# Bank assignment of score tiles and value products in the memory attention of a hybrid encoder step

## The chip, the cores and the metric

The kernel runs on one core of one Trainium2 chip. The metric is the device time of one execution in microseconds (us); the time given for a kernel is the median of its runs. A profile is one further execution, recorded by the hardware profiler; its span runs from the first to the last recorded instruction.

Engine names as in the profile: PE is TensorE (matmuls), PEld its weight loads, DVE VectorE, ACT ScalarE, POOL GpSimd, SP the engine whose queue issues most DMAs. PSUM, where matmuls write, has eight banks of 512 float32 values per partition.

## The reference

One layer of an encoder is applied to 512 prompt tokens and 64 sample tokens, with shared weights: a mixing block (a gated delta recurrence beside a differential attention), a cross-attention to a memory of 256 rows, and a feed-forward block; then a final norm. The change concerns the cross-attention:

```python
def _mem_attn(x, mk, mv, wq, wo):                      # x: rmsnorm(h)
    q = (x @ wq).reshape(B, L, H_MEM, D_MEM)            # 4 heads of width 256
    s = jnp.einsum('blhd,bmhd->bhlm', q, mk) * (D_MEM ** -0.5)
    p = jax.nn.softmax(s, axis=-1)                      # over 256 memory rows
    o = jnp.einsum('bhlm,bmhd->blhd', p, mv)
    return o.reshape(B, L, D_MODEL) @ wo
```

For the prompt, mk and mv are projected from the memory input; for the sample they come from a cache.

## The kernel before, in words

**Layout.** Activations lie transposed: model dimension on the 128 partitions (eight blocks of 128), the 576 tokens along the free axis. A matmul of near-float32 accuracy is made of three matmuls on operands split into a high and a low part (float32r each): high by high, low weight by high, high weight by low. `project` (L169) computes one 128-wide block of outputs for all tokens in two halves: tokens 0 to 255 in one bank (eight contraction steps k; at each, the high weights go over the high and low activations side by side, 512 columns in one matmul, and the low weights over 256 columns), then tokens 256 to 575 (eight steps of three matmuls with 320 columns). A projection is thus 16 + 24 = 40 matmuls. Its weights arrive by DMA as `raw` (three buffers) and are split by ACT (`wh`, L161) and DVE (`wl`, L162), two buffers each.

**The memory attention** is a loop over four heads h (L1151 on). For each head:

- two projections give the head's queries, evacuated and split by `split_query` (high part L1160 on ACT, low part `ql` L1161 on DVE, both after L194 and L195 for the first half);
- five score tiles t, one for each 128 tokens of the prompt and one for the sample. A tile is six matmuls of 256 columns into a bank `gs`; then DVE takes the row maximum (L1178) and scales it (L1179), ACT takes the exponential and its sum out of the bank (L1181), DVE takes the reciprocal (L1182) and scales the row (L1183). The bank is free after the exponential. PE transposes the 128 by 256 probabilities as two blocks into a bank `ba` (L113); for a prompt tile ACT casts each block to its high part (L1190) and DVE subtracts to get the low part (L1191); for the sample tile DVE copies (L1193, tile `an` in the profile). The probability tile `p0` has two buffers;
- two value products i, one for each 128 of the head's 256 columns: six matmuls of 512 columns for the prompt tokens into `b`, four of 64 columns for the sample into `b2`; both are evacuated and split into the tile pair `mo` by ACT (L1209) and DVE (L1210).

After the loop, `project` is called for the eight blocks of w_mem_o over `mo` (the contraction steps k = 2h and 2h + 1 need head h), each followed by the residual add (`add_residual`, L1092 and L1094) and `combine`, which prepares operands of the feed-forward block. `split_first` and `load_pair` (L1262) prepare the first weights of that block on DVE, ACT and the DMA queue.

**Banks.** PSUM is given out by tag:

```python
BANKS = dict(pr=3, ba=2, g0=1, g1=1, gs=1)
```

A tag with n banks hands out n tiles in turn; the next tile waits until the oldest has been read for the last time. `project` uses `pr`, the transposes use `ba`, score tiles `gs`, value products `g0` and `g1`. The feed-forward block later uses `ba`, `gs` and `g1` for its seven products (`ff1_pair`).

**Order.** The framework puts each engine's instructions into one fixed order when the program is built, by simulating their costs: what comes earlier in the program has priority, and what is not ready yet lets later work pass. (The splitting of weights has a raised priority.) On the chip each engine runs its list in order, and an instruction whose operands or bank aren't ready holds up all behind it. So within head h PE's list mixes the head's score matmuls, transposes and value products with the projections of head h + 1, the next work in the program. In the last head, h = 3, there are no queries left to project; what can be mixed in are the first projections of w_mem_o, as far as their contraction steps k = 0 to 5 (heads 0 to 2) and the three `pr` banks reach.

Of the kernel before, what the change touches and what calls it, by code (L numbers as in the profile page):

```python
# [37 lines left out]
def hybrid_layer_kernel(  # L38
# [40 lines left out]
    def nm(s):  # L79
        uid[0] += 1  # L80
        return f"{s}_{uid[0]}"

    def pair(slot, dt=F32):

        return up.tile([P, 2, 4, T], dt, tag=f"u{slot}", name=nm("u"))
# [6 lines left out]
    def small(tag, shape, bufs=None, dt=F32):  # L92
        tag = SHARED.get(tag, tag)
        bufs = 1 if tag in ("vn", "on", "S") or tag[:-1] in ("At", "Dt", "Y") else 2
        return sp.tile(shape, dt, tag=tag, name=nm(tag), bufs=bufs)

    def tiny(shape, tag="tiny", bufs=16):
        return tp.tile(shape, F32, tag=tag, name=nm(tag), bufs=bufs)

    def bank(tag="ba"):  # L100
        return ps.tile([P, 512], F32, tag=tag, name=nm(tag), bufs=BANKS[tag])
# [4 lines left out]
    def mm(out, lhsT, rhs, start=True, stop=True, pin=False, skip_group_check=False):  # L106
        i = nc.tensor.matmul(out, lhsT, rhs, start=start, stop=stop, skip_group_check=skip_group_check)  # L107
        if pin:
            tc.keep_in_program_order(i)

    def tr(out, in_, pin=False):
        n = in_.shape[0]
        i = nc.tensor.transpose(out, in_, ident[:n, :n])  # L113
        if pin:
            tc.keep_in_program_order(i)
# [49 lines left out]
    def weights(w, c0, kt=KT):  # L165

        return split_weights(w[:, c0 : c0 + P], [P, kt, P])

    def project(w, x, evac, kt=KT, halves=HALVES, between=None):  # L169


        for a0, n in halves:
            b = bank("pr")
            for k in range(kt):
                low_part = lambda: mm(b[:, :n], w[1][:, k, :], x[k // 4][:, 0, k % 4, a0 : a0 + n], start=False, stop=False)
                if k == kt - 1:
                    low_part()
                high_parts(b, w[0], x, k, a0, n, kt)
                if k < kt - 1:
                    low_part()  # L180
            if between and a0 == 0:
                between()
            evac(b[:, :n], a0, n, None if a0 else b[:, 256:])
# [9 lines left out]
    def add_to(dst, b, more):  # L193
        A.copy(dst, more)  # L194
        V.tensor_tensor(dst, b, dst, ALU.add)  # L195
# [298 lines left out]
    for a0, n in HALVES:  # L494
        b = bank("pr")
# [7 lines left out]
    b = bank()  # L503
# [67 lines left out]
    for j in range(3):  # L571
        b = bank()
# [456 lines left out]
    def lows(*tags):  # L1029

        return [small(tag, [P, 512], dt=F32R) for tag in tags]
# [9 lines left out]
    for w, out in ((w_mem_k, o_mk), (w_mem_v, o_mv)):  # L1041
        dst = tokens
        for f in range(2):
# [17 lines left out]
            if out is o_mk:  # L1061
                for i in range(2):
                    b = bank()
# [79 lines left out]
    for k2 in range(KT // 2):  # L1143
        b = bank()
# [6 lines left out]
    for h in range(H):  # L1151
        qh = [small("kd" if h % 2 else "aT", [P, T], dt=F32R) for i in range(2)]
        ql = cp.tile([P, 2, T], F32R, tag=f"qz{h % 2}", name=nm("ql"))
        for i in range(2):
            def split_query(b, a0, n, more):
                if more is not None:
                    q = small("zr", [P, 320])[:, :n]
                    add_to(q, b, more)
                    b = q
                A.copy(qh[i][:, a0 : a0 + n], b)  # L1160
                V.tensor_tensor(ql[:, i, a0 : a0 + n], b, qh[i][:, a0 : a0 + n].bitcast(F32), ALU.subtract)  # L1161

            project(weights(w_mem_q[0], (2 * h + i) * P), hx, split_query)

        pT = [lows(*tags) for tags in ((("p1", "p1"), ("S", "vn")) if h % 2 else (("vb", "vb"), ("KQ", "KQ")))]
        pS = small("an", [P, 2, DEC])
        for t, (q0, _) in enumerate(QT):
            t0, n = TT[t]
            kk, kl = (mkT, mkl) if t < 4 else (cmT, cml)
            b = bank("gs")  # L1170
            for i in range(2):
                m, q = 2 * h + i, slice(q0, q0 + P)
                low_keys = kl[m // 2][:, m % 2, :]
                mm(b[:, :NMEM], qh[i][:, q], kk[:, m, :], start=i == 0, stop=False)
                mm(b[:, :NMEM], qh[i][:, q], low_keys, start=False, stop=False)
                mm(b[:, :NMEM], ql[:, i, q], kk[:, m, :], start=False, stop=i == 1)
            mx, l = tiny([P, 1]), tiny([P, 1])
            V.tensor_reduce(mx, b[:, :NMEM], AX.X, ALU.max)  # L1178
            V.tensor_scalar(mx, mx, shrink16[:, t : t + 1], None, ALU.mult)  # L1179
            p = small("p0", [P, 512])  # L1180
            A.activation(p[:, :NMEM], b[:, :NMEM], AF.Exp, bias=mx, scale=grow16[:, t : t + 1], accum_out=l)  # L1181
            V.reciprocal(l, l)  # L1182
            V.tensor_scalar(p[:, :NMEM], p[:, :NMEM], l, None, ALU.mult)  # L1183
            bt = bank()
            for bi in range(2):
                tr(bt[:, bi * P : (bi + 1) * P], p[:, bi * P : (bi + 1) * P])
            if t < 4:
                for bi in range(2):
                    src, (dh, dl) = bt[:, bi * P : (bi + 1) * P], (x[bi][:, t0 : t0 + n] for x in pT)
                    A.copy(dh, src)  # L1190
                    V.tensor_tensor(dl, src, dh.bitcast(F32), ALU.subtract)  # L1191
            else:
                V.tensor_copy(pS, bt[:, : 2 * P].rearrange("p (b n) -> p b n", b=2)[:, :, P - n :])  # L1193
        if h % 2 == 0:
            mo.append(pair(4 if h else 5, F32R))
        for i in range(2):
            b, b2 = bank("g0"), bank("g1")
            fs = slice((2 * h + i) * P, (2 * h + i + 1) * P)
            for bi in range(2):
                m = 2 * h + i  # L1200
                mm(b, mv[:, bi, fs], pT[0][bi], start=bi == 0, stop=False)
                mm(b, mv[:, bi, fs], pT[1][bi], start=False, stop=False)
                mm(b, mvl[2 * bi + m // 4][:, (m % 4) * P : (m % 4 + 1) * P], pT[0][bi], start=False, stop=bi == 1)
            for bi in range(2):
                mm(b2[:, :DEC], cmv[2 * bi + m // 4][:, (m % 4) * P : (m % 4 + 1) * P], pS[:, bi, :], start=bi == 0, stop=bi == 1)
            j = 2 * (h % 2) + i
            for src, ts_ in ((b, slice(0, SEQ)), (b2[:, :DEC], slice(SEQ, T))):
                dh, dl = (mo[h // 2][:, p, j, ts_] for p in range(2))
                A.copy(dh, src)  # L1209
                V.tensor_tensor(dl, src, dh.bitcast(F32), ALU.subtract)  # L1210
# [322 lines left out]
    for m in range(KT):  # L1533
# [3 lines left out]
        if m in (3, 4):  # L1537
            t = m - 3
# [43 lines left out]
```

## Time and profile before

| | us |
|---|---|
| median of 3 runs (lowest, highest) | 1025.71 (1025.43, 1027.94) |
| profiled execution, its own time | 1028.23 |
| its span | 1026.5 |
| PE busy in the span | 1003.6 (98%) |
| PE weight loads | 921.1 (90%) |
| DVE busy | 706.8 (69%) |
| ACT busy | 537.0 (52%) |
| POOL busy | 57.1 (6%) |
| memory attention, first score matmul to the wait behind the last value product | 485.42 to 574.41 |

The profiled execution lies 2.52 us above the median and 1.73 us above its own span. All times with a position, such as 551.1, are us from the start of the span. A row of the table of windows gives a stretch, its length and the busy time of each engine with the number of instructions, then the granted TensorE clock (PEclk, 1.00 is full speed). Ends of matmuls are modelled, so that two in sequence overlap in the listing; the distance from start to start is the pace. A bracket at a row's end is the engine's idle time before it and what ended it. The profile names tiles by their tag: `u` is the big activation pairs, `aT` and `kd` the high queries of even and odd heads, `g` the banks `g0` and `g1`.

### The profile page before, as it was taken

What the parts mean: (1) busy time and instruction counts of PE and PEld (TensorE: products, weight loads), DVE (VectorE), ACT (ScalarE), POOL (GpSimd) and SP (SyncE); (2) the same over time, 40 slices, a digit from 0 to 9 for tenths busy, and PEclk for the clock granted to TensorE, in tenths of its full rate; (3) what the DMA queues carried; (4) which work ended last, traced back from release to release, by engine and by line L of the source; (5) the groups of instructions that cost most, each with busy time, mean ns of one, the idle gap of its engine ahead of it and who ended that gap; (6) DMA issues with size and microseconds to landing.
All of it is one profiled execution on the core that took longest, in us unless ns stands there. A gap on an engine that the chain in (4) does not pass through costs nothing.

```text
span 1026.5 us, 17294 instructions
## 1 busy us (share of the span) xinstructions
PE 1003.6 (98%) x6630; PEld 921.1 (90%) x6630; DVE 706.8 (69%) x1529; ACT 537.0 (52%) x1170; POOL 57.1 (6%) x123
## 2 busy tenths in 40 slices
PE   9999999999999999999999999999999999999996
PEld 7989899998888877899988899999999999999986
DVE  6576785776566676665665787667766677777883
ACT  6654664343465665444444557655544555555434
POOL 3431010100000000000000000000000000000000
PEclk9999999999999999999999999999999999999998
DMA  7332320100312355523211233332222222222202
GB/s 217 122 104 78 107 74 21 44 21 22 104 53 75 100 177 189 172 84 115 62 42 42 62 114 93 114 93 83 83 83 83 83 83 83 82 83 83 82 1 93
DMA packets 121255, 89.99 MB, mean 88 GB/s; under 512 B 5507, under 2 KB 112129, under 8 KB 120661
## 3 DMA queue, kind: packets, MB, share of 16 engines
q1 hardware_dynamic: 120804, 88.24, 28.6%
q8 instruction: 52, 0.85, 0.3%
q10 hardware_dynamic: 368, 0.66, 0.2%
q14 instruction: 31, 0.25, 0.1%
HBM read 79.14 MB, written 9.74 MB: 87 GB/s over the span
## 4 chain that ended last, share of the span: by engine, by line
PE 84%; DVE 4%; issue 3%; ACT 3%; POOL 2%; DMA 1%; POOLq 0%; ACTq 0%; DVEq 0%; SPq 0%
PE pr L107 49%; PE g L107 14%; PE ba L107 10%; PE gs L107 7%; PE ba L113 2%; PE g L113 2%; DVE wl L162 0%; DMA raw<-in_w_ff_dram 0%; POOL tg L208 0%; DVE p L457 0%; DMA out_dram<-S 0%; DMA S<-in_state_gdn_dram 0%; POOL X L604 0%; DMA r<-in_w_ff_dram 0%; DVE on L780 0%
## 5 line engine op out<-in xcount | busy, mean ns | idle before, releaser
L107 PE MATMUL pr<-u,wh 128*128 128x320 f32 (+2 forms) x1240 | 328.2, 342 | 2.1 <-DVE p L323 1.0
L107 PEld LDWEIGHTS pr<-u,wh 128*128 128x128 f32 x1240 | 211.6, 188 | 18.6 <-DVE p L323 1.3
L107 PE MATMUL pr<-u,wl 128*128 128x256 f32 (+1 forms) x816 | 227.7, 303 | 0.0
L107 PEld LDWEIGHTS pr<-u,wl 128*128 128x128 f32 x816 | 149.7, 189 | 3.7 <-issue 0.7
L162 DVE TENSOR_TENSOR wl<-raw,wh 128x1024 fp32r<-128x1024 f32 x65 | 79.5, 1223 | 34.4 <-ACT wh L161 32.5
L107 PE MATMUL pr<-u,w2h 128*128 128x320 f32 (+1 forms) x384 | 99.2, 343 | 2.8 <-DVE u L1415 2.8
L161 ACT CAST wh<-raw 128x1024 fp32r<-128x1024 f32 x65 | 68.2, 1049 | 58.0 <-PE pr L107 52.2
L1330 ACT CAST w2h<-r 128x512 fp32r<-128x512 f32 x56 | 34.7, 620 | 93.6 <-PE pr L107 89.9
L107 PE MATMUL pr<-f,w2h 128*128 128x320 f32 (+1 forms) x288 | 73.8, 340 | 0.0
L107 PEld LDWEIGHTS pr<-u,w2h 128*128 128x128 f32 x384 | 65.9, 191 | 7.9 <-DVE u L1415 3.1
L107 PE MATMUL pr<-u,w2l 128*128 128x256 f32 (+1 forms) x256 | 65.8, 298 | 0.0
L1415 DVE TENSOR_TENSOR u<-u,pr 128x256 f32<-128x256 f32 x96 | 42.9, 449 | 18.5 <-PE pr L107 17.6
L107 PE MATMUL ba<-u,wl 128*128 128x288 f32 x360 | 52.9, 295 | 0.6 <-ACT keep L1366 0.5
L107 PEld LDWEIGHTS pr<-f,w2h 128*128 128x128 f32 x288 | 48.7, 188 | 4.2 <-issue 1.2
L107 PEld LDWEIGHTS ba<-u,wl 128*128 128x128 f32 x360 | 49.2, 188 | 1.2 <-ACT keep L1366 1.2
L107 PEld LDWEIGHTS pr<-u,w2l 128*128 128x128 f32 x256 | 47.5, 191 | 1.5
L107 PE MATMUL pr<-f,w2l 128*128 128x256 f32 (+1 forms) x192 | 48.8, 295 | 0.0
L1331 DVE TENSOR_TENSOR w2l<-r,w2h 128x512 fp32r<-128x512 f32 x56 | 38.5, 688 | 11.3 <-ACT w2h L1330 10.8
L208 POOL TENSOR_TENSOR tiny<-tiny,nhalf 128x1 f32<-128x1 f32 (+4 forms) x10 | 9.2, 924 | 633.7 <-DVE tiny L1479 542.0
L107 PE MATMUL pr<-wh,u 128*128 128x512 f32 x128 | 41.2, 400 | 0.0
L107 PEld LDWEIGHTS pr<-f,w2l 128*128 128x128 f32 x192 | 35.2, 188 | 1.1
L1375 ACT ACTIVATE c<-c 128x288 f32<-128x288 f32 x48 | 20.9, 442 | 28.1 <-DVE c L1374 28.1
(462 smaller groups left out, 2078.5 us busy)
## 6 DMA issues: line engine op xcount, KB each, us to landing
raw<-in_w_ff_dram SPq DMA_DIRECT2D x36, 512.0 KB
raw<-in_w_in_dram SPq DMA_DIRECT2D x28, 512.0 KB
r<-in_w_ff_dram SPq DMA_DIRECT2D x56, 256.0 KB
raw<-in_w_mem_k_dram SPq DMA_DIRECT2D x8, 512.0 KB
raw<-in_w_mem_v_dram SPq DMA_DIRECT2D x8, 512.0 KB
raw<-in_w_out_dram SPq DMA_DIRECT2D x8, 512.0 KB
raw<-in_w_mem_q_dram SPq DMA_DIRECT2D x8, 512.0 KB
raw<-in_w_mem_o_dram SPq DMA_DIRECT2D x8, 512.0 KB
```

What stands on the lines that cost most here:

```text
L107: i = nc.tensor.matmul(out, lhsT, rhs, start=start, stop=stop, skip_group_check=skip_group_check)
L113: i = nc.tensor.transpose(out, in_, ident[:n, :n])
L161: A.copy(wh, raw)
L162: V.tensor_tensor(wl, raw, wh.bitcast(F32), ALU.subtract)
L208: G.tensor_tensor(out, in_, bc(nhalf[: in_.shape[0], 0:1], list(in_.shape)), ALU.pow)
L1330: A.copy(wh, src)
L1331: V.tensor_tensor(wl, src, wh.bitcast(F32), ALU.subtract)
L1375: A.activation(c, c, AF.Relu)
L1415: V.tensor_tensor(am, am, b, ALU.add)
```

## The change

Two lines of the memory attention name other banks. The score tiles t = 0 to 4 of a head take `gs`, `g0`, `g1`, `gs`, `g0`. The value product i = 0 has its prompt part in `g0` and its sample part in `g1` as before; i = 1 has its prompt part in `gs` and its sample part in one of the two `ba` banks. No matmul, no instruction of another engine and no DMA is added or removed; `BANKS` stays as it is.

```diff
         for t, (q0, _) in enumerate(QT):
             t0, n = TT[t]
             kk, kl = (mkT, mkl) if t < 4 else (cmT, cml)
-            b = bank("gs")
+            b = bank(("gs", "g0", "g1")[t % 3])
             for i in range(2):
                 m, q = 2 * h + i, slice(q0, q0 + P)
                 low_keys = kl[m // 2][:, m % 2, :]
...
         if h % 2 == 0:
             mo.append(pair(4 if h else 5, F32R))
         for i in range(2):
-            b, b2 = bank("g0"), bank("g1")
+            b, b2 = bank(("g0", "gs")[i]), bank(("g1", "ba")[i])
             fs = slice((2 * h + i) * P, (2 * h + i + 1) * P)
             for bi in range(2):
                 m = 2 * h + i
```

## The prediction

> **What bounds the kernel now.** I read the page first: busy time by engine, then the chain that ended last.
>
> ```profile
> span 1026.5 us, 17294 instructions
> PE 1003.6 (98%) x6630; PEld 921.1 (90%) x6630; DVE 706.8 (69%) x1529; ACT 537.0 (52%) x1170; POOL 57.1 (6%) x123
> PE 84%; DVE 4%; issue 3%; ACT 3%; POOL 2%; DMA 1%; POOLq 0%; ACTq 0%; DVEq 0%; SPq 0%
> ```
>
> PE is busy 98% of the span and is 84% of the chain. The change removes no matmul, so it can only win where PE idles or runs slowly in the memory attention. The table of windows with one stretch for each head, cut at the head's first score matmul (the last ends behind PE's last wait), shows where that is:
>
> ```profile
> 485.42:507.20 21.78, 21.78 (x142) 19.77 (x141) 13.49 (x41) 10.59 (x30) 0.00 (x0) 1.00 0.17 49
> 507.20:529.10 21.90, 21.90 (x142) 19.79 (x141) 13.56 (x42) 10.57 (x30) 0.00 (x0) 1.00 0.17 49
> 529.10:550.98 21.88, 21.88 (x143) 19.74 (x141) 12.77 (x41) 10.54 (x30) 0.00 (x0) 1.00 0.17 49
> 550.98:574.41 23.43, 20.69 (x119) 17.46 (x117) 13.06 (x41) 9.22 (x27) 0.00 (x0) 0.93 0.07 23
> ```
>
> In heads 0 to 2 PE is busy all of the time at full clock: the next head's 80 projection matmuls fill every wait for a bank. Only head 3 has a hole: 23.43 - 20.69 = 2.74 us idle, and a clock of 0.93. PE's windows inside it and its listing tell what happens:
>
> ```profile
> 562.00:563.00 1.00, 0.09 (x1) 1.00 0.00 0
> 563.50:564.00 0.50, 0.34 (x2) 0.81 0.00 0
> 564.00:565.00 1.00, 1.00 (x6) 0.50 0.00 0
> 565.00:566.00 1.00, 0.86 (x4) 0.50 0.00 0
> 566.00:567.00 1.00, 1.00 (x3) 0.50 0.00 0
> 567.00:567.50 0.50, 0.50 (x3) 0.78 0.00 0
> ```
> ```profile
> 551.89 0.42 DVE L1178 TENSOR_REDUCE tiny<-gs 128x1 f32<-128x256 f32 x1 [0.15 <-PE gs L107]
> ...
> 560.82 0.39 PE L107 MATMUL gs<-u,kd 128*128 128x256 f32 x1
> ...
> 561.41 0.44 PE L113 MATMUL ba<-ident,p 128*128 128x128 f32 x2
> ...
> 562.13 0.42 DVE L1178 TENSOR_REDUCE tiny<-gs 128x1 f32<-128x256 f32 x1 [0.77 <-PE gs L107]
> 562.67 0.20 DVE L1179 TENSOR_SCALAR tiny<-tiny,ta 128x1 f32<-128x1 f32 x1
> 562.95 0.57 ACT L1181 ACTIVATE p<-gs,tiny,ta 128x256 f32<-128x256 f32 x1
> 563.66 0.69 PE L107 MATMUL gs<-u,kd 128*128 128x256 f32 x2 [1.57 <-ACT p L1181]
> ...
> 568.42 0.29 DVE L1193 COPY an<-ba 128x128 f32<-128x128 f32 x1 [0.68 <-PE ba L113]
> 568.76 0.43 PE L107 MATMUL g<-an,X 128*128 128x64 f32 x2 [0.38 <-DVE an L1193]
> ...
> 569.72 0.41 PE L107 MATMUL pr<-u,wh 128*128 128x320 f32 x1 [0.30 <-ACT u L1209]
> 569.97 0.40 PE L107 MATMUL g<-p,u 128*128 128x512 f32 x1
> ...
> 574.41 0.56 PE L107 MATMUL pr<-u,wh 128*128 128x320 f32 x2 [0.30 <-DVE u L1092]
> ```
>
> The last score tile waits for the one bank `gs`, which the exponential of the tile before frees: 2.84 us from tile to tile (560.82 to 563.66), 1.57 of it idle, with the filler used up. The clock then falls to half until 567.2, which costs 3 x 0.50 + 0.5 x 0.22 + 0.5 x 0.19 = 1.7 us. The sample's copy holds PE 0.38 us, and value product i = 1 begins at 569.97, behind the eviction of i = 0.
>
> The Trainium skill, page "TensorE: Matmul & The Clock Gate", section "HAM oscillation — how this bites in real kernels", has idle gaps beyond about 3.4 us as what slows the clock. The trace disagrees, since 1.57 us was enough here; by the page's rule this stretch would hold 2.7 us to recover and not 4.4, and the measurement decides.
>
> **The change, part by part.** Nothing is added or dropped: 30 score matmuls, 10 transposes, 20 value matmuls a head, and the same work on ACT and DVE. No DMA moves; SP and POOL have nothing in the changed lines.
>
> *Ceiling.* What would head 3 take with PE always fed? Head 2 does, and the two differ in filler alone: 80 matmuls against 56 (contraction steps 0 to 7 of two first halves and one second half of w_mem_o), so 24 matmuls of 320 columns fewer.
>
> ```profile
> 529.10 0.28 PE L107 MATMUL gs<-u,aT 128*128 128x256 f32 x1
> 529.81 0.40 PE L107 MATMUL pr<-u,wh 128*128 128x512 f32 x1
> 530.04 0.28 PE L107 MATMUL pr<-u,wl 128*128 128x256 f32 x1
> 530.16 0.39 PE L107 MATMUL pr<-u,wh 128*128 128x512 f32 x1
> ...
> 534.02 0.31 PE L107 MATMUL pr<-u,wl 128*128 128x320 f32 x1
> 534.17 0.46 PE L107 MATMUL pr<-u,wh 128*128 128x320 f32 x2
> 534.46 0.31 PE L107 MATMUL pr<-u,wl 128*128 128x320 f32 x1
> ```
>
> From start to start: a score tile 0.71 us, a step of a first half 0.35, a step of a second half (three matmuls) 0.44. So 24 matmuls are 8 x 0.44 = 3.5 us, the fed head 3 takes 21.88 - 3.5 = 18.4 us, and 23.43 - 18.4 = 5.0 us is the most that can be won. The items read off above give 2.74 + 1.7 = 4.4.
>
> *Score tiles over three banks.* What replaces the wait for the bank is the softmax itself. Its price on DVE and ACT:
>
> ```profile
> L1178 DVE TENSOR_REDUCE tiny<-gs 128x1 f32<-128x256 f32 x5 | 2.1, 423 | 2.6 <-PE gs L107 2.6
> L1183 DVE TENSOR_SCALAR p<-p,tiny 128x256 f32<-128x256 f32 x5 | 1.8, 354 | 0.2
> L1191 DVE TENSOR_TENSOR KQ<-ba,vb 128x128 fp32r<-128x128 f32 x8 | 2.3, 285 | 0.2 <-ACT vb L1190 0.2
> L1179 DVE TENSOR_SCALAR tiny<-tiny,ta 128x1 f32<-128x1 f32 x5 | 1.0, 204 | 0.0
> L1182 DVE RECIPROCAL tiny<-tiny 128x1 f32<-128x1 f32 x5 | 0.8, 163 | 1.8 <-ACT p L1181 1.8
> L162 DVE TENSOR_TENSOR wl<-raw,wh 128x1024 fp32r<-128x1024 f32 x2 | 2.5, 1226 | 0.5 <-ACT wh L161 0.5
> L1161 DVE TENSOR_TENSOR ql<-pr,aT 128x320 fp32r<-128x320 f32 x1 | 0.5, 483 | 0.0
> L1181 ACT ACTIVATE p<-gs,tiny,ta 128x256 f32<-128x256 f32 x5 | 2.8, 569 | 2.0 <-DVE tiny L1179 2.0
> ```
>
> DVE: five tiles are 2.1 + 1.0 + 0.8 + 1.8 + 2.3 and one copy of 0.29, 8.3 us; with one weight split (1.2) and one query eviction (0.5), which pass it, 10.0 us. ACT has less (its largest row is 2.8). From head 3's first reduction at 551.89 the chain can thus end at 551.9 + 10.0 = 561.9 if DVE never waits; before, the copy ended at 568.7. The trace doesn't show three tiles in flight. At best it is 561.9, at worst each tile still takes its 2.84 us and nothing is won. I take 2 us of gaps (DVE and ACT read the transposed tile in turn, and only two `p0` and two `ba` buffers exist): 564.
>
> PE's cover until then, from 550.98: scores 5 x 0.71 = 3.6, filler 6 x (0.35 + 0.35 + 0.44) = 6.8, transposes about 5 x 0.3 = 1.5 (estimate: a pair's row has 0.44, which overlaps its neighbours), then the prompt's value matmuls, which need only tiles 0 to 3: 12 of 0.23 (the pace of 512 columns), 2.8. Together 14.7, to 565.7: PE need not wait for the sample's copy at 564. If that cover is gone (chain later than 565.7), each us late is a us lost and, beyond about 1.5, the clock's 1.7 too.
>
> *Value products in banks of their own.* Product i = 1 no longer waits for the eviction of i = 0. This is part of the idle 2.74 above (0.38 + 0.30), not an extra term. What is late next is the eviction of i = 1, ahead of contraction step 7 of w_mem_o; the sample's matmuls and step 6 (0.35 + 0.35 + 0.44 = 1.1 us) lie beside it.
>
> *Waits added.* Score tiles 1 and 4 now share a bank with i = 0, tiles 0 and 3 with i = 1. A head's first score tile must wait for the last eviction of the head before; behind it on PE would stand tile 1 and filler. In heads 0 to 2 earlier tiles let the products end earlier, with the rest of the projections between them and the next head. So from nothing to 1.6 us a head, the longest wait for a bank seen here; I take nothing, since at 529.81 and after it filler stands ready.
>
> *Sum.* Of 4.4 us I leave 0.3 for the last wait (`u` L1092 at 574.41), which stays: 4.1 us. Heads 0 to 2 stay full; their periods differ by 0.12, so 3 x 0.12 = 0.4 either way. Behind 574.41 PE is fed, so the shift should carry. The profiled execution would go from 1028.23 to 1024.1; the median, 2.52 below it, from 1025.71 to 1021.6.
>
> **Rivals.**
>
> *Half of it: the hole moves.* If the fixed order places tile 3 or 4, or a transpose, ahead of the filler and the chip is late there, PE still idles once and the clock halves again: 4.1 less 1.7 and about 0.6 of idle is 1.8; 1023.9. For it: PE's list waits for whatever stands first. Against: 6.8 us of filler.
>
> *No effect.* The softmax, not the bank, sets the pace, or filler is spent as before: 1025.7. For it: the 2.84 us can include weight splits that pass the softmax. Against: PE's wait at 563.66 is for the bank. The same section of the Trainium skill tells of a kernel whose PE was kept fed, where PSUM double-buffering gave no further gain (126.6 against 125.5 us); by that rule this rival holds, which the trace bears out for heads 0 to 2, where PE has no wait, and not for head 3.
>
> *Slower: the projections' evictions starve.* Packed softmax work stands ahead of the next head's evictions (L195, L1161) in DVE's list, the three `pr` banks fill, and PE idles in heads 0 to 2, where it doesn't now. It decides once an eviction comes later than the two other banks last: 8 x 0.35 + 8 x 0.44 = 6.3 us of projection plus what PE has of its own (scores 3.6), 9.9 us. A packed softmax of 10.0 us that let no eviction pass would just reach that. Price: about 1.5 us idle and 1.7 of clock in each of three heads, 9.6, less the 4.1 won: 5.5 slower, 1031.2. Against: DVE is busy 13.5 of 21.9 us a head, and evictions would find gaps.
>
> **How the numbers follow.** About 0.3% (3.1 us) is what a measurement of this kernel can tell from no change. The hole closes (1021.6, own range 1020.0 to 1022.6): 0.5. It moves: 0.15. No effect: 0.15. Slower: 0.2, since the new order is unknown. So faster 0.5, same 0.3, slower 0.2. The low end is the ceiling with the scatter: 1025.71 - 5.0 - 0.4 - 0.3 (between the two lower runs) = 1020.0. The high end, 1030.0, takes in half of the slower case.
>
> **What would show it.** Right: in head 3 no PE wait for `p` L1181, clock 1.00, 18.4 to 19.5 us from its first score matmul to the last wait, the copy `an` some 13 us behind the first score matmul instead of 17.4. Wrong: PE waits on evictions of `pr` in heads 0 to 2, a clock under 1.00 there, or the hole at another tile.

## The result, and the profile after

Over 12 runs of each, the changed kernel takes 1024.71 us (1023.26 to 1026.73) against 1026.83 us (1025.43 to 1028.50): a ratio of 0.9976, with a 95% interval of 0.9967 to 0.9984. Two later comparisons, on two chips, gave 0.9976 (0.9967 to 0.9985) and 0.9975 (0.9964 to 0.9985). So the change gains 0.24%, where 0.4% was forecast (4.1 of 1025.71 us). The profiled execution took 1024.58 us.

From the page of the changed kernel, the rows that answer to the first ones of before:

```profile
span 1022.9 us, 17296 instructions
PE 1002.1 (98%) x6630; PEld 921.1 (90%) x6630; DVE 703.3 (69%) x1529; ACT 535.3 (52%) x1170; POOL 57.1 (6%) x123
```

The table of windows, cut at the same instructions as before. The first three stretches end at the next head's first score matmul; the last ends at the matmul that waited at 574.41 before, the 57th that head 3's stretch puts into `pr`:

```profile
485.91:507.39 21.48, 21.48 (x142) 19.59 (x141) 12.96 (x41) 10.21 (x30) 0.00 (x0) 1.00 0.17 50
507.39:528.95 21.56, 21.56 (x142) 19.57 (x141) 13.00 (x41) 10.20 (x30) 0.00 (x0) 1.00 0.17 50
528.95:550.53 21.58, 21.58 (x142) 19.56 (x141) 12.29 (x40) 10.11 (x30) 0.00 (x0) 1.00 0.17 49
550.53:568.58 18.05, 18.05 (x119) 16.06 (x118) 13.49 (x43) 10.32 (x29) 0.00 (x0) 1.00 0.10 30
```

The hole of head 3 is gone: PE is busy for all 18.05 us, where the same work took 23.43, and the clock stays at 1.00. The sample's copy in DVE's listing stands 11.1 us behind the head's first score matmul, where it stood 17.4 us behind it:

```profile
561.62 0.29 DVE L1193 COPY an<-ba 128x128 f32<-128x128 f32 x1 [0.41 <-PE ba L113]
```

So far more was won than the end shows. Two more windows for each kernel tell where it went: from head 0's first score matmul to the first product of the feed-forward block (`ba<-B,w`), and from there to the first product of that block's fourth pair (`ba<-B,wh`; a pair is one call of `ff1_pair`, seven products). Where a few of a product's twelve matmuls ran ahead of the rest, the cut is at the rest. First before, then after:

```profile
485.42:616.34 130.92, 128.18 (x803) 116.33 (x802) 89.71 (x233) 66.07 (x157) 0.00 (x0) 0.99 0.22 63
616.34:664.63 48.29, 47.35 (x334) 45.40 (x332) 36.97 (x63) 34.44 (x78) 0.00 (x0) 1.00 0.36 106
```
```profile
485.91:610.18 124.27, 124.27 (x803) 114.16 (x801) 86.65 (x233) 64.19 (x157) 0.00 (x0) 1.00 0.23 66
610.18:660.92 50.74, 48.65 (x335) 47.02 (x333) 36.49 (x63) 34.73 (x78) 0.00 (x0) 0.97 0.35 101
```

The memory attention and the w_mem_o projections take 130.92 - 124.27 = 6.65 us less. The first part of the feed-forward block then takes 2.45 us more, though the change has no line in it. In that part PE waits once, and the clock falls behind the wait. From the list of waits, PE's listing and PE's windows of the changed kernel:

```profile
PE ba L107 <- ACT keep L1366: 2.0, 1, 2.0
```
```profile
628.40 2.21 PE L107 MATMUL ba<-u,wl 128*128 128x288 f32 x12 [2.04 <-ACT keep L1366]
```
```profile
628.00:630.00 2.00, 1.60 (x11) 0.92 0.52 153
630.00:632.00 2.00, 2.00 (x10) 0.50 0.38 109
632.00:634.00 2.00, 2.00 (x13) 0.73 0.00 0
```

PE waits 2.04 us for `keep`, ACT's eviction of the second pair's first product, and runs at half clock after it. ACT's listing says why `keep` is late, and SP's listing why the load is:

```profile
626.07 0.62 ACT L1330 CAST w2h<-r 128x512 fp32r<-128x512 f32 x1 [1.97 <-DMA r<-in_w_ff_dram]
626.59 0.43 ACT L1380 CAST u<-c 128x288 fp32r<-128x288 f32 x1
626.92 0.61 ACT L1330 CAST w2h<-r 128x512 fp32r<-128x512 f32 x1
627.44 0.61 ACT L1229 CAST wh<-s 128x512 fp32r<-128x512 f32 x1
627.96 0.39 ACT L1366 COPY keep<-ba 128x288 f32<-128x288 f32 x1
```
```profile
618.12 1.92 SPq L1262 DMA_DIRECT2D raw<-in_w_ff_dram  x2
620.09 8.91 SPq L1336 DMA_DIRECT2D r<-in_w_ff_dram  x5
```

ACT waited for `r`, a 256 KB load of w_ff2 for the second output block, and four instructions later came to `keep`. The load had been issued behind two loads of 512 KB. Before, the same load went out ahead of both, at once when its buffer came free:

```profile
624.27 0.37 SPq L1336 DMA_DIRECT2D r<-in_w_ff_dram  x1
624.87 1.98 SPq L1262 DMA_DIRECT2D raw<-in_w_ff_dram  x2
```

Nobody wrote that order. The build lays out every queue by simulated times, and with the memory attention changed it came out differently. On DVE two instructions changed places: `w2l` of L1331, for which the load waited in before (it frees the load's buffer), stood ahead of the subtraction of L1288, for which the bigger loads wait (623.55 and 624.16); now it stands behind it. DVE's listing of the changed kernel:

```profile
617.37 0.68 DVE L1288 TENSOR_TENSOR raw<-raw,raw 128x512 f32<-128x512 f32 x1
617.97 0.69 DVE L1331 TENSOR_TENSOR w2l<-r,w2h 128x512 fp32r<-128x512 f32 x1
```

That this swap is what put the load behind its neighbours in SP's queue fits the waits, but no run shows it by itself.

### The profile page after: what moved, and what is told of

Its sections match the earlier page's. It is cut to its first block, busy times and chain, and to the rows that moved or that the text cites. A ratio compares the mean times of both kernels' runs of the same rounds, so it can differ in the third digit from the quotient of the medians.

```text
span 1022.9 us, 17296 instructions
## 1 busy us (share of the span) xinstructions
PE 1002.1 (98%) x6630; PEld 921.1 (90%) x6630; DVE 703.3 (69%) x1529; ACT 535.3 (52%) x1170; POOL 57.1 (6%) x123
## 4 chain that ended last, share of the span: by engine, by line
PE 84%; DVE 3%; issue 3%; ACT 2%; POOL 2%; DMA 1%; POOLq 0%; ACTq 0%; DVEq 0%; SPq 0%
PE pr L107 49%; PE g L107 14%; PE ba L107 10%; PE gs L107 7%; PE ba L113 2%; PE g L113 2%; DMA r<-in_w_ff_dram 1%; DVE wl L162 0%; POOL tg L208 0%; DVE p L457 0%; DMA out_dram<-S 0%; DMA S<-in_state_gdn_dram 0%; POOL X L604 0%; DVE on L780 0%; ACT L645 0%
## 5 line engine op out<-in xcount | busy, mean ns | idle before, releaser
L1331 DVE TENSOR_TENSOR w2l<-r,w2h 128x512 fp32r<-128x512 f32 x56 | 38.5, 688 | 11.7 <-ACT w2h L1330 11.5
```

Source lines behind the costliest of these rows:

```text
L1331: V.tensor_tensor(wl, src, wh.bitcast(F32), ALU.subtract)
```

## The experiments

All ratios are to the kernel before, measured beside it on the same chip, with the 95% interval. Two lengths from each profile stand beside them: A, from head 0's first score matmul to the feed-forward block's first product, and B, from there to its fourth pair.

| kernel | ratio (interval) | A, us | B, us | PE's wait for `keep` in B, us |
|---|---|---|---|---|
| before | 1 | 130.92 | 48.29 | 0.9 |
| the change | 0.9976 (0.9967 to 0.9984) | 124.27 | 50.74 | 2.0 |
| e1, score tiles only | 0.9932 (0.9919 to 0.9944) | 124.43 | 47.93 | 0.4 |
| e2, value products only | 0.9984 (0.9974 to 0.9993) | 129.62 | 47.96 | 0.5 |
| e3, the change, load early | 0.9940 (0.9926 to 0.9953) | 124.31 | 48.28 | 0.6 |
| e4, the change, loads by POOL | 0.9998 (0.9989 to 1.0008) | 124.33 | 55.18 | 5.5 |
| e5, score tiles over two banks | 0.9951 (0.9939 to 0.9964) | 125.16 | 47.91 | 0.5 |
| e6, before, load early | 1.0001 (0.9992 to 1.0010) | 129.99 | 47.76 | 0.4 |
| e7, the change again | 0.9976 (0.9967 to 0.9985) | 124.30 | 50.40 | 3.0 |
| e8, score tiles only, load early | 0.9948 (0.9935 to 0.9960) | 124.40 | 47.73 | 0.4 |
| e9, score tiles only, load late | 0.9945 (0.9931 to 0.9959) | 124.46 | 47.83 | 0.5 |
| e10, before, load late | 1.0012 (1.0003 to 1.0020) | 130.09 | 48.34 | 0.9 |
| e11, score tiles only, again | 0.9936 (0.9924 to 0.9949) | 124.45 | 47.93 | 0.5 |
| e12, the change, load early, again | 0.9941 (0.9928 to 0.9955) | 124.87 | 47.96 | 0.5 |
| e13, the change, eviction first | 0.9931 (0.9918 to 0.9945) | 124.29 | 47.71 | none |
| e14, the change, third time | 0.9975 (0.9964 to 0.9985) | 124.30 | 53.98 | 4.3 |

**One half of the change at a time.**

e1:
```diff
-            b = bank("gs")
+            b = bank(("gs", "g0", "g1")[t % 3])
```


> Only the score tiles take three banks in turn; both value products stay in g0 and g1. Theory (the wait of the last score tile for its bank was the hole of head 3, and the changed kernel closes it but gives 2 to 3 us back where the feed-forward block begins, because there one weight load of SP's queue is placed behind two loads of twice its size): here that queue keeps the order of the kernel before, so the time should be below the changed kernel's, 1021 to 1023.5 us, the feed-forward block begin 5 to 6 us earlier than before, and PE wait under 1 us at its start. Rival (the feed-forward block's first weights can't come earlier, whatever the queue's order): the block begins earlier by the same 5 to 6 us, PE waits 2 us or more there, and the time is 1024 to 1025.

e2:
```diff
-            b, b2 = bank("g0"), bank("g1")
+            b, b2 = bank(("g0", "gs")[i]), bank(("g1", "ba")[i])
```


> Only the value products get banks of their own; the score tiles stay in one bank. Theory: the wait for the score bank in head 3 (1.57 us) and the halved clock behind it stay, and at most the 0.38 and 0.30 us around the value products go: 0 to 1 us faster than before, 1025.8 to 1027. Rival (the value products set the pace of the tail): 3 us or more faster than before.

The score tiles alone give the whole gain in A (6.5 of 6.65 us) and keep B: 1021.48 against 1028.78 us, 0.68% faster, and better than the full change. The value products alone gain 0.16% (1027.18 us), a little more than the expected 0 to 1 us; the wait for the score bank stays, with a clock of 0.61 and 0.53 in the two stretches of 2 us from 564 on, and so does the last wait behind head 3. PE's listing of e2:

```profile
563.95 0.51 PE L107 MATMUL gs<-u,kd 128*128 128x256 f32 x2 [1.57 <-ACT p L1181]
573.53 0.56 PE L107 MATMUL pr<-u,wh 128*128 128x320 f32 x2 [0.29 <-DVE u L1092]
```

So the single bank of the score tiles was the hole. In e1 the load keeps its old place, which fits the theory without proving it: e1 has other differences of order too. SP's listing of e1:

```profile
618.18 0.37 SPq L1336 DMA_DIRECT2D r<-in_w_ff_dram  x1
618.78 1.98 SPq L1262 DMA_DIRECT2D raw<-in_w_ff_dram  x2
```

**The late load moved forward.**

e3, and e12 the same again:
```diff
         raw = ft("r2", [P, 4, P], 3)
-        nc.sync.dma_start(raw, w[:, c0 : c0 + P].rearrange("(k p) n -> p k n", p=P))
+        with tc.high_priority():
+            nc.sync.dma_start(raw, w[:, c0 : c0 + P].rearrange("(k p) n -> p k n", p=P))
```


> The changed kernel, and the loads of w_ff2 are issued at a raised priority, so that the second of them stands in SP's queue ahead of the last of the two bigger loads. Theory (the place in the queue costs the 2 us wait and the slow clock behind it): the wait of PE at the start of the feed-forward block falls below 1 us, the clock there stays at 1.00, and the time is 2 to 2.5 us below the changed kernel's, 1022 to 1023. Rival (the order of ACT and DVE work there, not the load, sets the wait): as the changed kernel, 1024 to 1025.5.

e6 (the same edit on the kernel before) and e8 (on the score tiles alone):

> The kernel before with the loads of w_ff2 at a raised priority: the control for the same edit on the changed kernel. There the second load stands ahead of both bigger loads already. Theory (the edit repairs only the place that the change had spoiled): within 0.1% of before. Rival (the edit is worth something by itself): 0.2% or more faster than before.

> Three banks for the score tiles, value products as before, and the loads of w_ff2 at a raised priority. Theory (the load is in its place already with the score tiles alone): as the kernel with the score tiles alone, 0.65 to 0.72% faster than before. Rival (the raised priority wins more): 0.8% or more.

The edit takes the changed kernel from 0.9976 to 0.9940, B from 50.74 to 48.28 us, with the clock at 1.00 all through B. The kernel before gains nothing by it (1.0001). e8's 0.9948 is below the expected 0.65% gain, with an interval that overlaps those of e1 and e11; its A and B are theirs, so the difference isn't explained by anything in these stages. In e3 the load goes out second, and lands early enough:

```profile
619.09 0.37 SPq L1262 DMA_DIRECT2D raw<-in_w_ff_dram  x1
619.66 0.37 SPq L1337 DMA_DIRECT2D r<-in_w_ff_dram  x1
620.65 0.37 SPq L1262 DMA_DIRECT2D raw<-in_w_ff_dram  x1
```

**The loads in another queue.**

e4:
```diff
         raw = ft("r2", [P, 4, P], 3)
-        nc.sync.dma_start(raw, w[:, c0 : c0 + P].rearrange("(k p) n -> p k n", p=P))
+        nc.gpsimd.dma_start(raw, w[:, c0 : c0 + P].rearrange("(k p) n -> p k n", p=P))
```


> The changed kernel, and all loads of w_ff2 are issued by POOL, which is idle in the feed-forward block, so that none stands behind another in SP's queue. Theory (a load held up in SP's queue costs the wait): no wait of 2 us at the start of the feed-forward block, 1022 to 1023, if POOL's queue costs nothing of its own. Rival (the load's own 3 us and the order on ACT set the wait): as the changed kernel, 1024 to 1025.5, or above it if the issue on POOL is late.

This one failed: 1028.24 us, level with before, B 55.18 us. POOL issued the load at 619.29, which is earlier than the changed kernel's 620.09, but ACT's cast of it could begin only at 626.63. Rows of e4: POOL's issue, ACT's wait and PE's.

```profile
619.29 0.79 POOL L1336 DMA_DIRECT2D r<-in_w_ff_dram  x1 [62.11 <-DVE w2l L1331]
```
```profile
626.63 0.62 ACT L1330 CAST w2h<-r 128x512 fp32r<-128x512 f32 x1 [4.60 <-DMA r<-in_w_ff_dram]
```
```profile
632.08 2.29 PE L107 MATMUL ba<-u,wl 128*128 128x288 f32 x8 [5.50 <-ACT keep L1366]
```

A queue of its own didn't help the load that ran beside two bigger ones: 7.3 us from issue to cast, against 3.1 us in before (624.27 to 627.34, where ACT waited for it too). POOL's queue as such is not slow: of its six loads issued from 600 to 660 this one took longest to land, 7.3 us, and the median is 3.4. So it isn't the wait in SP's queue alone, but the big loads ahead of it or beside it, that make it late.

**The load moved back on purpose.**

e9 (on the score tiles alone) and e10 (on the kernel before); `pair_loads` holds the instructions of the bigger loads:
```diff
         raw = ft("r2", [P, 4, P], 3)
-        nc.sync.dma_start(raw, w[:, c0 : c0 + P].rearrange("(k p) n -> p k n", p=P))
+        with tc.issue_after(pair_loads[3, 0]) if late else ExitStack():
+            nc.sync.dma_start(raw, w[:, c0 : c0 + P].rearrange("(k p) n -> p k n", p=P))
...
-            project(weights2(w_ff2[0, (g - 1) * 512 : g * 512, :], m * P), (pend,), add_group(g - 1, m), kt=4)
+            project(weights2(w_ff2[0, (g - 1) * 512 : g * 512, :], m * P, g == 1 and m == 1), (pend,), add_group(g - 1, m), kt=4)
```


> The score tiles alone over three banks, and the second load of w_ff2 tied behind the two bigger loads in SP's queue, where the changed kernel has it; nothing else differs from the score tiles alone. Theory (that place gives the time back): PE waits 2 us or more where the feed-forward block begins, and the gain over the kernel before falls from 0.5 to 0.7% to 0.2 to 0.4%. Rival (something else in the changed kernel's order gives it back): as the score tiles alone, no wait above 1 us.

> The kernel before with the same load tied behind the two bigger ones. Theory: 1.5 to 4 us slower than before, a wait of PE of 2 us or more where the feed-forward block begins. Rival: no difference.

Here the theory as it stood fell. e9 has the changed kernel's order of loads, yet no wait above 0.5 us and B 47.83 us. e10 loses 0.12% only, 0.8 us, with a wait of 0.9. The load of e9 is as late as in the changed kernel, but ACT's listing has another order:

```profile
624.32 0.39 ACT L1368 COPY keep<-ba 128x288 f32<-128x288 f32 x1
626.28 0.62 ACT L1331 CAST w2h<-r 128x512 fp32r<-128x512 f32 x1 [1.57 <-DMA r<-in_w_ff_dram]
```

Where the build knew of the tie, it placed the eviction `keep` of the second pair's first product ahead of the cast, in e10 too (630.73 and 633.09). ACT still waits 1.57 us for the load in e9, and PE then waits only 0.51 us for ACT, for a later eviction.

**The eviction ahead of the cast.** This leads to the second theory: the late load costs because the cast of it stands ahead of the eviction. e13 leaves the code of the loads as it is in the changed kernel and ties that one weight's cast behind the eviction of the third pair's first product (`keeps` holds it). That puts it behind the second pair's too, for which PE waited in the changed kernel. e14 is the changed kernel, measured beside e13 on one chip.

```diff
-        return split(raw, "w2", 3)
+        with tc.issue_after(keeps[2]) if behind else ExitStack():
+            return split(raw, "w2", 3)
...
         s1 = keep(x)
+        keeps[p] = nc.cur_bb.bb.instructions[-1]
...
-            project(weights2(w_ff2[0, (g - 1) * 512 : g * 512, :], m * P), (pend,), add_group(g - 1, m), kt=4)
+            project(weights2(w_ff2[0, (g - 1) * 512 : g * 512, :], m * P, g == 1 and m == 1), (pend,), add_group(g - 1, m), kt=4)
```


> The changed kernel with one edit on ACT's order: the cast of the second w_ff2 load stands behind the eviction of the third pair's first product, not ahead of it; SP's queue keeps the changed kernel's order, so the load lands as late as there. Theory (the late load costs only because ACT's cast of it stands ahead of the eviction that PE waits for): no wait of PE above 1 us where the feed-forward block begins, 0.5 to 0.7% faster than before. Rival (the late load costs in any order): a wait of 2 us or more, 0.2 to 0.35% faster.

> The changed kernel beside the one with the eviction first, on one chip. Theory: 0.2 to 0.3% faster than before, the wait of 2 to 3 us as in its other profiles, 0.3% or more behind the other. Rival: level with the other.

> The changed kernel once more, beside the others on one chip. Theory: 0.2 to 0.3% faster than before, some 0.4% behind the kernels that keep the load in its place; PE's wait of 2 us and the slow clock at the start of the feed-forward block again. Rival (the first result was off): 0.5% or more faster than before.

e13 takes 1021.44 us and e14 1025.72, both against 1028.21. In e13 the late load stands behind the two bigger ones as in the changed kernel (loads after it come later, as the casts free their buffers later), the second pair's eviction is on time, and PE has no wait in B at all. SP's and ACT's listings of e13, and all of PE's waits from the memory attention to the end:

```profile
617.69 1.92 SPq L1262 DMA_DIRECT2D raw<-in_w_ff_dram  x2
619.66 2.46 SPq L1336 DMA_DIRECT2D r<-in_w_ff_dram  x3
```
```profile
623.91 0.39 ACT L1367 COPY keep<-ba 128x288 f32<-128x288 f32 x1
```
```profile
PE pr L107 <- DVE u L1417: 2.8, 1, 2.8
PE pr L107 <- DVE u L1419: 0.2, 1, 0.2
```

The three profiles of the changed kernel also show how unsteady a wait for a load is. The load was issued at 620.09, 620.38 (e7) and 620.64 (e14), its cast began at 626.07, 627.29 and 628.88, and PE waited 2.0, 3.0 and 4.3 us. The slow clock that was expected of e7 did not come. ACT's listing of e14, then PE's wait and windows of e7:

```profile
628.88 0.62 ACT L1330 CAST w2h<-r 128x512 fp32r<-128x512 f32 x1 [4.24 <-DMA r<-in_w_ff_dram]
```
```profile
629.65 1.87 PE L107 MATMUL ba<-u,wl 128*128 128x288 f32 x12 [2.99 <-ACT keep L1366]
```
```profile
630.00:632.00 2.00, 2.00 (x16) 1.00 0.75 213
```

**Is a third bank needed, and the value products' own?**

e5:
```diff
-            b = bank("gs")
+            b = bank(("gs", "g0")[t % 2])
```


> The score tiles in turn over two banks only (gs and g0), the value products in g0 and g1 as before. Theory (one tile must be computed while another's softmax runs; DVE's 10 us of softmax, not the number of banks, is the limit beyond that): head 3's hole closes as with three banks, 0.6 to 0.7% faster than before, at most 1 us behind three banks. Rival (three tiles in flight are needed to cover the latency): PE waits for a score bank in head 3 again, and the gain is 0.3% or less.

> The score tiles alone over three banks once more, for a comparison on one chip. Theory: 0.5 to 0.7% faster than before. Rival (the first result was luck of the chip): 0.4% or less.

> The changed kernel with the loads of w_ff2 at a raised priority once more, beside the score tiles alone. Theory (the banks of the value products are worth nothing beyond the score tiles): within 0.15% of the score tiles alone. Rival (they are worth the 0.7 us of the waits seen in head 3): 0.5 us or more faster than the score tiles alone at the start of the feed-forward block.

Two banks close the hole: no wait for a score bank, clock 1.00, A 125.16 us, 0.7 behind three banks. The gain of 0.49% is somewhat below the 0.6 to 0.7% expected. With two banks heads 0 to 2 take about as long as before; with three they are shorter. PE's windows of e5, then of e1:

```profile
485.78:507.54 21.76, 21.76 (x143) 1.00 0.17 49
507.54:529.30 21.76, 21.76 (x142) 1.00 0.17 49
529.30:551.26 21.96, 21.96 (x142) 1.00 0.16 49
```
```profile
485.82:507.20 21.38, 21.38 (x142) 1.00 0.18 50
507.20:528.76 21.56, 21.56 (x142) 1.00 0.17 50
528.76:550.52 21.76, 21.76 (x142) 1.00 0.17 49
```

The full change with the load early (e3, e12: 0.9940, 0.9941) and the score tiles alone (e1, e11: 0.9932, 0.9936) don't differ beyond their intervals. Banks of their own for the value products are worth nothing that can be measured once the score tiles have theirs. The best of all are e1 and e13, about 0.65 to 0.7% faster than before.

## Why the prediction was wrong

**What bounds the kernel, and the hole: right.** PE's wait for the score bank in head 3 was the place, as e2 (it stays with one bank) and e1 (it goes with three) show. Heads 0 to 2 had no wait and got none. The copy `an` came even earlier than forecast, 11.1 us behind the head's first score matmul instead of 13.

**The rivals.** The hole did not move, the projections' evictions did not starve, and the change had an effect. The time came out near the rival "half of it", by another mechanism than the one it names.

**The gain in the memory attention: mis-sized, too small.** 5.0 us was given as the most that head 3 could win, and 4.1 were taken. Head 3 won 23.43 - 18.05 = 5.4 us. About 1.0 of it belongs to the clock in that one execution of before (22.47 us in e6; next point). The last wait of 0.30 (`u` L1092), which was to stay, is gone too. With 0.3 us behind head 3, and 65.56 - 64.62 = 0.94 in heads 0 to 2 (485.42 to 550.98 before, 485.91 to 550.53 after), for which 0.4 either way was given, that makes the 6.65 us of A. Heads 0 to 2 were taken as fixed because PE was full in them; but a full PE still depends on the order of its matmuls. Both stretches hold the same matmuls. By the starts in PE's listing the 90 score matmuls among them take 12.8 us before and 11.6 after: 22 of them before, and 9 after, have 0.20 us or more to the next start, nearly all others 0.12. What in the order costs this isn't settled; that three banks shorten the heads and two hardly do is all that e1 and e5 show.

**The clock's 1.7 us: not a fixed price.** e6 has the kernel before unchanged in the memory attention, and the same idle stretch in head 3, with the clock at 1.00 all through. Before's rows, then e6's:

```profile
562.00:564.00 2.00, 0.43 (x3) 0.95 0.00 0
564.00:566.00 2.00, 1.86 (x9) 0.50 0.00 0
566.00:568.00 2.00, 2.00 (x6) 0.69 0.00 0
```
```profile
562.00:564.00 2.00, 0.43 (x4) 1.00 0.00 0
564.00:566.00 2.00, 1.76 (x11) 1.00 0.00 0
566.00:568.00 2.00, 1.62 (x9) 1.00 0.00 0
```

Yet e6's A is only 0.9 us shorter than before's:

```profile
485.39:615.38 129.99, 127.17 (x803) 115.12 (x802) 89.72 (x233) 65.98 (x157) 0.00 (x0) 1.00 0.22 63
```

PE is idle in it for 2.82 us, against 2.74 in before, and busy for 1.0 us less, not 1.7. Why the half clock cost less than that isn't settled. The prediction had one profile, with the slow clock, and took it for the rule; behind the same wait of 1.57 us e2 has the slow clock, e6 and e10 have it not. The Trainium skill, page "TensorE: Matmul & The Clock Gate", section "What's actually happening", says that the clock is set by a window of activity that runs freely and isn't started by the kernel; that the same wait is punished in one execution and not in another agrees with it. So do two profiles of the changed kernel: half clock behind PE's wait of 2.04 us, 1.00 behind 2.99 us in e7.

**The failed step: "Behind 574.41 PE is fed, so the shift should carry."** PE was full from there to 616.34 and nearly full behind it, and from that the prediction concluded that what came earlier would end earlier. But the feed-forward block's beginning had no margin: in before, ACT already waited for the same load (until its cast at 627.34), and PE for `keep` (0.9 us in all, in B). The change moved one load behind two bigger ones and left its cast ahead of an eviction; 2.45 us and more came back there, some of it as slow clock. e13 (0.9931, B 47.71 us, against e14's 0.9975 and 53.98 beside it) and e3 win this back, each by one edit outside the memory attention. The prediction said that "No DMA moves", which was true of the changed lines and false of the built order.

**Luck.** The profiled execution came out at 1024.58 us, where 1024.1 was forecast. That is two errors that nearly cancel, 6.65 us won in A for 4.1 and 2.45 given back in B for nothing; and both are read against a profile of before with the slow clock in head 3. The medians differ by 2.1 us.

## What to carry to other kernels

Where a planner fixes every queue's order at build time, an edit in one stage can reorder a load in the next one: compare the built orders of all engines and of the DMA queue, not only the lines of the diff, before believing or dismissing a small gain. An engine's instruction that waits for a load holds up all behind it; where evictions that the matmul engine needs stood ahead of it, the late load cost nothing that could be measured (e9 beside e11, e13). A stage in which the bound engine hardly idles may have no margin left; to ask whether an earlier start will carry through it, look at what its other engines wait for.

## What the runs showed of the hardware that was not expected

- The same idle gap of 1.57 us on PE was followed by about 3.4 us of half clock in the profile of before (0.19 + 3.00 + 0.22, worked out from the windows of 563.5 to 567.5) and by none in e6's. In the changed kernel a wait of 2.04 us was followed by half clock, one of 2.99 us (e7) by none.
- A load of 256 KB issued at 619.29 in a queue of its own, beside two of 512 KB, could be used only at 626.63, 7.3 us later; ahead of them it took 3.1 us (624.27 to 627.34 in before).
- The same load in the same order was usable 6.0, 6.9 and 8.2 us after its issue in three executions of the changed kernel (626.07, 627.29 and 628.88).
